# Modulation products in the attention stage: two more weight buffers, loads on GpSimd's queue tied to the present unit, products two half tiles behind

## The chip, the cores and the metric

The kernel runs on one core of a Trainium2 chip. The metric is the device time of one execution in microseconds (us). The core has the engines TensorE (PE in the profile, its weight loads PEld), VectorE (DVE), ScalarE (ACT), GpSimd (POOL) and SyncE (SP, which only issues transfers here). Each takes its instructions in a fixed order, and an instruction whose inputs or whose buffer is not ready holds up all that stand behind it on the same engine.

## The reference, cut to what matters

One layer for 512 latent tokens and 256 context tokens of width 2048, in fp32: a normalisation modulated by the vector `c`, one input projection, four heads of gated linear attention beside a gated convolution, an output projection, and a gated feed-forward network.

```python
mx = jax.nn.silu(c) @ w_mod[i] + b_mod[i]            # 2048 -> 6 x 2048
sh1, sc1, gt1, sh2, sc2, gt2 = split(mx, 6)
hx = modulate(rmsnorm(x, norm1_g), sh1, sc1)
q, k, v, g, lf, lb, cb, cc, cx = split_proj(hx @ w_in)
la_f = log_sigmoid(lf @ w_gate_f + b_gate_f) / 16    # forget gates, la_b alike
o_x = gla_bidir(q, k, v, la_f, la_b, s_f, s_b)       # four heads
mix = concat(o_x * silu(g), cb * conv(cc * cx)) @ w_out
x = x + gt1 * mix
h2 = modulate(rmsnorm(x, norm2_g), sh2, sc2)
x = x + gt2 * swiglu(h2)
```

The change concerns the last four of the six parts of `mx` (gt1, sh2, sc2, gt2: 8192 numbers, each a dot product of 2048 terms) and the forget gates of the latent tokens. The four parts are first needed when the output projection is added to `x`, so their computation is spread over the attention stage.

## The kernel before, in words

Weights come from memory as raw fp32 tiles of 128x1024 (512 KB) in a ring of four `raw` buffers (`load_raw`, line 115, on SP's queue). `load_w` (line 121) splits such a tile in two: ScalarE casts it to `whi` (line 102), VectorE computes the rest `wlo` = raw - whi (line 103). `whi` and `wlo` have three buffers each. TensorE then makes three matmuls for each product (`mm3`, line 92). A projection of 128 columns needs two such tiles; `proj_units` (line 465) calls each a unit, and a unit is 24 matmuls of 128x512.

The attention stage is a sequence of three calls of `weave` (line 528): the context's gates and states (`do_ctx`) beside two projections; the latent gates (`do_gates`, line 549) beside `do_g(0)` and `do_conv(0)`; then each of the four heads (`do_gla`, line 557) beside the projections of later heads and of the convolution. One step of `weave` emits one stage of the attention, one unit, and `mod_some(0.85, 64)`.

`mod_some` (line 367) computes the four parts of `mx` on VectorE. The weights `wm2` are laid out as 64 tiles of 128x2048; a tile comes in two halves of 128x1024, and each half is multiplied by the broadcast `cbc` = silu(c) and summed along its row by one instruction (line 374, `tensor_tensor_reduce`; the profile names it CUSTOM_DVE_ANT_0, and a second short instruction of the same line reads the sum out to `modacc`). The two halves of a tile are loaded and multiplied one directly after the other, in two `raw` buffers of the same ring that the unit weights use, on the same SP queue. Below, "product" means this VectorE instruction of line 374 unless matmuls are named.

Inside a head, TensorE's order is fixed by the program: the score matmuls into `psc` (line 598), VectorE's masked copy of them (line 599, `copy_predicated` into `hbig`), the state updates `pd` (line 618) which reuse a PSUM bank that the masked copy frees, `sn` on VectorE (line 621), `sm` on ScalarE (line 613), and the outputs `po` (line 625). The order of all instructions on each engine is fixed when the program is built; the transfer queues start what stands in them in order.

Scratch for `do_ctx` comes from a pool `hcpool`; it is closed after the context (line 537), and a pool `gp` is opened for gates and heads (line 541). The loop over the heads is at lines 669 to 675, the rest of the modulation at 676 to 679.

Of the kernel before, what the change touches and what calls it, by code (L numbers as in the profile page):

```python
# [7 lines left out]
F32 = mybir.dt.float32  # L8
# [3 lines left out]
ALU = mybir.AluOpType  # L12

P = 128
# [39 lines left out]
def tile_hybrid_block(  # L54
# [14 lines left out]

    es_ep = ExitStack()  # L70
    epool = es_ep.enter_context(tc.tile_pool(name="epool", bufs=1, side="right"))


    def big(dtype=F32):
# [40 lines left out]
    def load_raw(src):  # L115
        n = src.shape[-1]
        r = wpool.tile([P, 1024], F32, tag="raw", name="raw", bufs=4)
        nc.sync.dma_start(r[:, :n], src)
        return r[:, :n]

    def load_w(src, k, eng=None):

        r = load_raw(src)
        n = r.shape[-1]
        hi = wpool.tile([P, 1024], F32R, tag="whi", name="whi", bufs=3)
        lo = wpool.tile([P, 1024], F32R, tag="wlo", name="wlo", bufs=3)
        split(hi[:, :n], lo[:, :n], r, eng)
        return (hi[:, :n].rearrange("p (k n) -> p k n", k=k),
                lo[:, :n].rearrange("p (k n) -> p k n", k=k))
# [34 lines left out]
    gsc2 = cpool.tile([P, KD], F32, name="gsc2")  # L164
    cbc = epool.tile([P, D], F32, name="cbc")
    cstt = epool.tile([P, NBLK, P], F32, name="cstt")
    gatet = epool.tile([33, 2, 512], F32, name="gatet")
    lfT = epool.tile([33, SEQ + CTX], F32, name="lfT")
    maskt = epool.tile([P, 2, SEQ], U8, name="maskt")
    ident, ones, one16 = cidt[:, B_ID, :], cidt[:, B_ONE, :], cstt[:, B_ONE16, :]  # L170
    onecol = cidt[:, B_ONE, 0:1]
# [1 line left out]

    es_hc = ExitStack()
    hcpool = es_hc.enter_context(tc.tile_pool(name="hcpool", bufs=1, side="right"))

    ccolt = hcpool.tile([P, KD, 2], F32, name="ccolt")  # L180
    silsh = hcpool.tile([P, 2, KD, 32], F32, tag="lg", name="silsh")
# [182 lines left out]
    nc.scalar.activation(cbc, cbc, AF.Silu)  # L364
    nmod, owed = [0], [0.0]

    def mod_some(n, last):

        owed[0] += n
        while owed[0] >= 1 and nmod[0] < last:  # L370
            j = nmod[0]
            for hf in range(2):
                w = load_raw(wm2[j][:, hf * 1024 : hf * 1024 + 1024])
                nc.vector.tensor_tensor_reduce(  # L374
                    out=w, in0=w, in1=cbc[:, hf * 1024 : hf * 1024 + 1024], scale=1.0, scalar=0.0,
                    op0=ALU.mult, op1=ALU.add, accum_out=modacc[:, j, hf : hf + 1])
            nmod[0] += 1
            owed[0] -= 1

    MOD_STEP = 0.85  # L380

# [83 lines left out]
    def proj_units(acc, wsrc, x, units=(0, 1), part=ALL):  # L465

        for n, u in enumerate(units):
            w = load_w(wsrc[u], 8)
            for k in range(8):
                mm3(acc[:, part], sl(w, ALL, k), sl(x[8 * u + k], ALL, part), n == 0 and k == 0, n == 1 and k == 7)  # L470
            yield
# [62 lines left out]
            mod_some(MOD_STEP, 64)  # L534

    weave(do_ctx(), (None for g in (do_q(0), do_q(1)) for _ in g))
    es_hc.close()


    es_g = ExitStack()  # L540
    gp = es_g.enter_context(tc.tile_pool(name="gp", bufs=1, side="right"))
    msk = []
    for d in range(2):
        t = hbig()
# [4 lines left out]
    def do_gates():  # L549
        for tt in range(NX):  # L550
            pzs = [bank("pzs") for _ in range(2)]
            for d in range(2):
                mm(pzs[d], tok(lfT, tt), gatet[:, d, :], True, True)
            log_gates(gp, "on", pzs, [las[0][tt], las[1][tt]])
            yield

    def do_gla(h):
# [108 lines left out]
        mix[8 + c] = y  # L666

    weave(do_gates(), (None for g in (do_g(0), do_conv(0)) for _ in g))
    for h in range(HEADS):
        fill = [do_conv(c) for c in (2 * h, 2 * h + 1) if c]  # L670
        if h + 1 < HEADS:
            fill.insert(0, do_g(h + 1))
        if h + 2 < HEADS:
            fill.insert(0, do_q(h + 2))
        weave(do_gla(h), (None for g in fill for _ in g))
    mod_some(64, 64)
    mod_finish(0, 64)
    nc.vector.tensor_scalar(gsc2, modv[:, 32:48], 1.0, None, op0=ALU.add)
    nc.vector.tensor_tensor(gsc2, gsc2, colt[:, C_G2 : C_G2 + KD], op=ALU.mult)
# [570 lines left out]
```

## Time and profile before

| | before |
|---|---|
| median of the 3 runs shown | 2343.65 us (2339.64 to 2347.67) |
| the profiled execution's own time | 2345.66 us |
| its span, first to last instruction | 2343.9 us |
| PE, PEld, DVE, ACT, POOL busy (whole span) | 96%, 76%, 71%, 43%, 6% |
| mean granted TensorE clock | 0.987 |
| first and last product of line 374 | 304.6 and 829.5 us |

How to read it: times in views are microseconds from the span's start. A row of a wait view gives the waiting instruction, the one that released it, the total, the number of times and the longest. In a timeline row, `[3.06 <-DVE hbig L599]` says that the engine stood idle for 3.06 us until VectorE's instruction of line 599 on tile `hbig` ended. PEclk is the share of TensorE's full clock that was granted. A view by windows gives busy time, with the number of instructions in brackets, for each stretch.

### The profile page before, as it was taken

The numbers are of one execution on the slowest core, as the hardware profiler recorded it, in microseconds if no ns is written. First come the engines' busy times: TensorE is split into PE (matmuls) and PEld (weight loads), VectorE is DVE, ScalarE is ACT, GpSimd is POOL, SyncE is SP. The second block draws the span as 40 slices with busy tenths as digits, with TensorE's granted clock in tenths as the row PEclk, the third lists the DMA queues.
The fourth block names the chain that finished last, engine by engine and source line by source line (L and its number), as shares of the span: only waits on it lengthen the run. The fifth ranks groups of instructions, "written<-read, shape, count | busy, mean of one in ns | idle before, by whom it ended". The sixth has DMA issues, their size and how long they took to land.

```text
span 2343.9 us, 27639 instructions
## 1 busy us (share of the span) xinstructions
PE 2253.0 (96%) x10232; PEld 1792.7 (76%) x10232; DVE 1666.7 (71%) x2046; ACT 1010.0 (43%) x1361; POOL 146.1 (6%) x190
## 2 busy tenths in 40 slices
PE   8999999899989999989999999999999999999996
PEld 4765667787867778768888888888888878888875
DVE  3566164655655757779888788878887867787888
ACT  3432155233232334485554555455545544433343
POOL 2433000000000000010000000000000000000001
PEclk9999999999989999999999999999999999999998
DMA  9774365665666654534434643464345585755634
GB/s 323 232 247 135 135 226 169 199 196 191 214 190 192 203 177 163 177 136 135 153 123 147 207 144 123 147 206 144 124 146 207 187 317 177 279 180 197 243 127 143
DMA packets 161619, 431.43 MB, mean 184 GB/s; under 512 B 17867, under 2 KB 38635, under 8 KB 161356
## 3 DMA queue, kind: packets, MB, share of 16 engines
q1 hardware_dynamic: 141612, 380.87, 49.1%
q0 software_dynamic: 8720, 28.58, 3.2%
q10 hardware_dynamic: 11152, 20.21, 2.3%
q8 instruction: 81, 1.33, 0.2%
q14 instruction: 54, 0.44, 0.1%
HBM read 380.82 MB, written 48.78 MB: 183 GB/s over the span
## 4 chain that ended last, share of the span: by engine, by line
PE 51%; DVE 5%; issue 1%; ACT 1%; POOL 0%; DMA 0%; POOLq 0%; SPq 0%; DVEq 0%; ACTq 0%
PE acc L90 50%; DVE wlo L103 2%; PE pt L996 1%; DMA raw<-wd 0%; DVE ch L812 0%; POOL out L1129 0%; DVE y L1108 0%; DVE ch L793 0%; ACT whi L102 0%; ACT h L924 0%; ACT big L909 0%; DVE y L1120 0%; DVE y L1119 0%; DVE u L832 0%; POOL hbig L907 0%
## 5 line engine op out<-in xcount | busy, mean ns | idle before, releaser
L102 ACT CAST whi<-ch 128x1024 fp32r<-128x1024 f32 x350 | 368.8, 1054 | 426.5 <-PE acc L90 362.5
L103 DVE TENSOR_TENSOR wlo<-ch,whi 128x1024 fp32r<-128x1024 f32 x350 | 426.0, 1221 | 135.9 <-ACT whi L102 134.7
L102 ACT CAST whi<-raw 128x1024 fp32r<-128x1024 f32 x252 | 264.2, 1052 | 421.9 <-PE acc L90 221.4
L103 DVE TENSOR_TENSOR wlo<-raw,whi 128x1024 fp32r<-128x1024 f32 x252 | 308.9, 1227 | 187.1 <-ACT whi L102 186.8
L374 DVE CUSTOM_DVE_ANT_0 raw<-raw,cbc 128x1024 f32<-128x1024 f32 x128 | 156.4, 1224 | 193.6 <-DMA raw<-wm 190.8
L90 PE MATMUL acc<-hhl,whi 128*128 128x512 f32 x640 | 200.4, 394 | 0.0
L90 PE MATMUL acc<-hhi,wlo 128*128 128x512 f32 x320 | 135.2, 424 | 16.0 <-DVE wlo L103 15.2
L90 PEld LDWEIGHTS acc<-hhl,whi 128*128 128x128 f32 x640 | 121.3, 190 | 27.7 <-issue 2.5
L90 PE MATMUL acc<-hlo,whi 128*128 128x512 f32 x320 | 127.6, 399 | 0.2 <-DVE hlo L108 0.2
L90 PE MATMUL acc<-whi,a5l 128*128 128x512 f32 x312 | 122.2, 392 | 5.7 <-DVE a5l L103 5.7
L90 PE MATMUL acc<-hhl,wlo 128*128 128x512 f32 x320 | 127.6, 399 | 0.0
L90 PE MATMUL acc<-hhi,whi 128*128 128x512 f32 x320 | 126.7, 396 | 0.0
L90 PE MATMUL acc<-wlo,a0h 128*128 128x512 f32 x312 | 123.3, 395 | 2.1 <-DVE wlo L103 2.1
L90 PE MATMUL acc<-wlo,a6h 128*128 128x512 f32 x312 | 121.6, 390 | 1.4 <-DVE wlo L103 1.4
L90 PE MATMUL acc<-whi,a0h 128*128 128x512 f32 x312 | 122.2, 392 | 0.0
L90 PE MATMUL acc<-whi,a6l 128*128 128x512 f32 x312 | 121.5, 390 | 0.7 <-ACT whi L102 0.4
L90 PE MATMUL acc<-wlo,a5h 128*128 128x512 f32 x312 | 122.0, 391 | 0.0
L90 PE MATMUL acc<-whi,a5h 128*128 128x512 f32 x312 | 121.8, 391 | 0.0
L90 PE MATMUL acc<-whi,a0l 128*128 128x512 f32 x312 | 121.8, 391 | 0.0
L90 PE MATMUL acc<-whi,a6h 128*128 128x512 f32 x312 | 121.4, 389 | 0.0
L90 PE MATMUL acc<-whi,a2l 128*128 128x512 f32 x280 | 108.9, 391 | 4.8 <-ACT whi L102 4.8
L90 PE MATMUL acc<-wlo,a2h 128*128 128x512 f32 x280 | 109.9, 393 | 1.2 <-DVE wlo L103 1.2
(307 smaller groups left out, 4749.5 us busy)
## 6 DMA issues: line engine op xcount, KB each, us to landing
raw<-wm SPq DMA_DIRECT2D x128, 512.0 KB, 4.8
raw<-wu SPq DMA_DIRECT2D x92, 512.0 KB, 4.4
ch<-wu SPq DMA_DIRECT2D x88, 512.0 KB, 3.9
raw<-wc SPq DMA_DIRECT2D x48, 512.0 KB, 3.8
raw<-wd SPq DMA_DIRECT2D x47, 512.0 KB, 6.0
ch<-wd SPq DMA_DIRECT2D x44, 512.0 KB, 5.8
opd<-oh ACTq DMA_DIRECT2D x77, 256.0 KB, 3.1
opd<-ol POOLq DMA_DIRECT2D x77, 256.0 KB, 3.3
```

What stands on the lines that cost most here:

```text
L90: nc.tensor.matmul(o, l, r, start=start, stop=stop, skip_group_check=True)
L102: nc.scalar.copy(hi, src)
L103: (eng or nc.vector).tensor_tensor(lo, src, hi, op=ALU.subtract)
L374: nc.vector.tensor_tensor_reduce(out=w, in0=w, in1=cbc[:, hf * 1024 : hf * 1024 + 1024], scale=1.0, scalar=0.0, op0=ALU.mult, op1=ALU.add, ...
L996: nc.tensor.transpose(pt[:, (2 * i + t) * P : (2 * i + t) * P + P], acts[j][2 * hf + t][:, q * P : q * P + P], ident)
```

## The change

It does five things.

1. `mod_some` now counts halves instead of whole tiles (`owed` grows by 2 x 0.85 = 1.7 a step), and a half may be loaded in one step and multiplied in a later one: loaded halves wait in the list `pend`.
2. From the first head on, `behind` is 2: a half is multiplied only after two later halves have been loaded.
3. From the first head on, loads are issued on GpSimd's queue instead of SP's. Of three halves two go to a new ring `wm` of two 128x1024 buffers in `gp`, one to the `raw` ring.
4. Ahead of each such load GpSimd copies one column of the present unit's `whi` into the buffer (128x1). The load then can't start before ScalarE has cast the present unit's weights and the buffer is free.
5. The latent gates are made in `hcpool`, in the tile that the context's gates used; `gatet` and `lfT` move into `hcpool` as well, which is closed after the gates, and `gp` is opened then.

During the context and the gates `behind` is 0: a half is loaded on SP's queue and multiplied at once, as before, but one half at a time. With 0.85 a step, about 27 halves fall in these 16 steps, and GpSimd issues the remaining 101.

```diff
-    gatet = epool.tile([33, 2, 512], F32, name="gatet")
-    lfT = epool.tile([33, SEQ + CTX], F32, name="lfT")
+    gatet = hcpool.tile([33, 2, 512], F32, name="gatet")
+    lfT = hcpool.tile([33, SEQ + CTX], F32, name="lfT")
...
+    pend, behind, unit = [], [0], []
+
     def mod_some(n, last):
-        owed[0] += n
-        while owed[0] >= 1 and nmod[0] < last:
-            j = nmod[0]
-            for hf in range(2):
-                w = load_raw(wm2[j][:, hf * 1024 : hf * 1024 + 1024])
-                nc.vector.tensor_tensor_reduce(
-                    out=w, in0=w, in1=cbc[:, hf * 1024 : hf * 1024 + 1024], scale=1.0, scalar=0.0,
-                    op0=ALU.mult, op1=ALU.add, accum_out=modacc[:, j, hf : hf + 1])
-            nmod[0] += 1
+        owed[0] += 2 * n
+        while owed[0] >= 1 and (pend or nmod[0] < 2 * last):
             owed[0] -= 1
+            if nmod[0] < 2 * last:
+                j, hf = divmod(nmod[0], 2)
+                src = wm2[j][:, hf * 1024 : hf * 1024 + 1024]
+                if behind[0] and nmod[0] % 3:
+                    w = gp.tile([P, 1024], F32, tag="wm", name="wm", bufs=2)
+                    nc.gpsimd.tensor_copy(w[:, 0:1], unit[0])
+                    nc.gpsimd.dma_start(w, src)
+                elif behind[0]:
+                    w = wpool.tile([P, 1024], F32, tag="raw", name="raw", bufs=4)
+                    nc.gpsimd.tensor_copy(w[:, 0:1], unit[0])
+                    nc.gpsimd.dma_start(w, src)
+                else:
+                    w = load_raw(src)
+                pend.append((j, hf, w))
+                nmod[0] += 1
+                if len(pend) <= behind[0]:
+                    continue
+            j, hf, w = pend.pop(0)
+            nc.vector.tensor_tensor_reduce(
+                out=w, in0=w, in1=cbc[:, hf * 1024 : hf * 1024 + 1024], scale=1.0, scalar=0.0,
+                op0=ALU.mult, op1=ALU.add, accum_out=modacc[:, j, hf : hf + 1])
...
             w = load_w(wsrc[u], 8)
+            unit[:] = [w[0][:, 0, 0:1].bitcast(F32)]
...
-            log_gates(gp, "on", pzs, [las[0][tt], las[1][tt]])
+            log_gates(hcpool, "lg", pzs, [las[0][tt], las[1][tt]])
...
     weave(do_gates(), (None for g in (do_g(0), do_conv(0)) for _ in g))
+    es_hc.close()
+    es_g = ExitStack()
+    gp = es_g.enter_context(tc.tile_pool(name="gp", bufs=1, side="right"))
+    behind[0] = 2
...
-    mod_some(64, 64)
+    mod_some(128, 64)
```

How the instructions stand, at three places. VectorE's order before, in the first head, around the masked copy (line 599); line 374 is the product on a `raw` tile `raw<-raw,cbc` and its read-out `modacc`, line 103 the `wlo` of a unit, line 621 the state update:

```order
L374 ISA raw,modacc<-raw,cbc 128x1024
L374 ISA modacc 128x1
L103 TENSOR_TENSOR wlo<-raw,whi 128x1024
L374 ISA raw,modacc<-raw,cbc 128x1024
L374 ISA modacc 128x1
L374 ISA raw,modacc<-raw,cbc 128x1024
L374 ISA modacc 128x1
L599 COPY_PREDICATED hbig<-maskt,psc 128x512 x2
L621 SCALAR_TENSOR_TENSOR sn<-s_2609,dc,pd 128x256
L601 TENSOR_TENSOR big<-hbig 128x512
L621 SCALAR_TENSOR_TENSOR sn<-s_2609,dc,pd 128x256
```

The same place on VectorE in the changed kernel, where line 395 is the product, line 107 the `wlo`, line 616 the masked copy, line 638 the state update, and `wm` the new ring:

```order
L395 ISA wm,modacc<-wm,cbc 128x1024
L395 ISA modacc 128x1
L107 TENSOR_TENSOR wlo<-raw,whi 128x1024
L395 ISA raw,modacc<-raw,cbc 128x1024
L395 ISA modacc 128x1
L616 COPY_PREDICATED hbig<-maskt,psc 128x512
L107 TENSOR_TENSOR wlo<-raw,whi 128x1024
L616 COPY_PREDICATED hbig<-maskt,psc 128x512
L638 SCALAR_TENSOR_TENSOR sn<-s_2609,dc,pd 128x256
L618 TENSOR_TENSOR big<-hbig 128x512
L638 SCALAR_TENSOR_TENSOR sn<-s_2609,dc,pd 128x256
```

Between the unit's `wlo` and the first masked copy stand two products before and one now, and the next unit's `wlo` has moved in between the two masked copies. The products that stand here now were loaded two halves earlier.

Directly behind the second `sn` of that place, VectorE's order in the changed kernel goes on so (`sn<-sn` is the next step's state update):

```order
L395 ISA wm,modacc<-wm,cbc 128x1024
L395 ISA modacc 128x1
L395 ISA wm,modacc<-wm,cbc 128x1024
L395 ISA modacc 128x1
L395 ISA raw,modacc<-raw,cbc 128x1024
L395 ISA modacc 128x1
L638 SCALAR_TENSOR_TENSOR sn<-sn,dc,pd 128x256 x2
```

Three products now stand between the two steps of the state; before there are a `wlo` and two products between them.

SyncE's queue before, in the first head: the weights of projections (`wq`, `wg`, `wc`) and those of the modulation (`wm`) alternate in the `raw` ring.

```order
L118 DMA raw<-wq 128x1024
L118 DMA raw<-wm 128x1024 x2
L118 DMA raw<-wg 128x1024
L118 DMA raw<-wm 128x1024 x2
L118 DMA raw<-wg 128x1024
```

GpSimd's queue in the changed kernel at its beginning in the heads: `COPY` is the column of the unit's `whi`, `DMA` the load (lines 386 and 387 for the `raw` ring, 382 and 383 for the `wm` ring).

```order
L386 COPY raw<-whi 128x1
L387 DMA raw<-wm 128x1024
L382 COPY wm<-whi 128x1 x2
L383 DMA wm<-wm 128x1024 x2
L386 COPY raw<-whi 128x1
L382 COPY wm<-whi 128x1
L387 DMA raw<-wm 128x1024
L383 DMA wm<-wm 128x1024
L382 COPY wm<-whi 128x1
L383 DMA wm<-wm 128x1024
```

SyncE keeps only the projections' weights in the heads; the modulation's loads stand on GpSimd's queue, where a load can stand behind the column copy of the next one. TensorE's order of instructions is the same in both kernels.

More of the change, by code (lines that the diff above doesn't have):

```diff
@@ L71, in tile_hybrid_block @@
     epool = es_ep.enter_context(tc.tile_pool(name="epool", bufs=1, side="right"))
+    es_hc = ExitStack()
+    hcpool = es_hc.enter_context(tc.tile_pool(name="hcpool", bufs=1, side="right"))
     def big(dtype=F32):
@@ L172, in tile_hybrid_block @@
     selt = smt[:, S_SEL : S_SEL + 2]
-    es_hc = ExitStack()
-    hcpool = es_hc.enter_context(tc.tile_pool(name="hcpool", bufs=1, side="right"))
     ccolt = hcpool.tile([P, KD, 2], F32, name="ccolt")
@@ L536, in tile_hybrid_block @@
     weave(do_ctx(), (None for g in (do_q(0), do_q(1)) for _ in g))
-    es_hc.close()
-    es_g = ExitStack()
-    gp = es_g.enter_context(tc.tile_pool(name="gp", bufs=1, side="right"))
     msk = []
```

## The prediction

> **What bounds the kernel now.** I read the busy times first, then a view by windows of the stage that the change touches, then who waited for whom there, then the two engines' timelines at one gap.
>
> The page's first part, and the windows: the attention stage from the second latent gate to the last head, six stretches inside it, and the rest of the kernel.
>
> ```profile
> PE 2253.0 (96%) x10232; PEld 1792.7 (76%) x10232; DVE 1666.7 (71%) x2046; ACT 1010.0 (43%) x1361; POOL 146.1 (6%) x190
> ...
> core 0: us, PE busy (x) PEld busy (x) DVE busy (x) ACT busy (x) POOL busy (x), PEclk, DMA share, GB/s
> 376.00:832.00 456.00, 420.20 (x1897) 343.83 (x1896) 272.99 (x461) 144.14 (x230) 0.00 (x0) 0.97 0.62 195
> 392.00:400.00 8.00, 6.64 (x22) 5.37 (x23) 3.60 (x4) 2.42 (x4) 0.00 (x0) 0.79 0.64 200
> 452.00:460.00 8.00, 6.24 (x19) 4.54 (x20) 5.66 (x10) 2.90 (x4) 0.00 (x0) 0.79 0.68 201
> 652.00:660.00 8.00, 3.89 (x14) 3.54 (x15) 5.97 (x13) 4.27 (x5) 0.00 (x0) 0.57 0.57 197
> 668.00:680.00 12.00, 9.80 (x30) 7.32 (x31) 7.76 (x14) 3.39 (x6) 0.00 (x0) 0.72 0.50 140
> 780.00:792.00 12.00, 8.13 (x26) 6.12 (x25) 10.21 (x20) 2.56 (x5) 0.00 (x0) 0.72 0.59 191
> 828.00:836.00 8.00, 6.44 (x21) 5.18 (x22) 7.84 (x15) 3.47 (x9) 0.00 (x0) 0.79 0.81 264
> 832.00:2343.00 1511.00, 1470.34 (x6548) 1211.10 (x6546) 1213.93 (x1315) 728.88 (x913) 66.17 (x113) 0.99 0.50 173
> ```
>
> TensorE is the bound, and in this stage it stands idle for 456.00 - 420.20 = 35.8 us. No other engine is full there: VectorE works 273 of 456 us, the transfers 62%, GpSimd does nothing. The six stretches are those where the clock fell: a busy TensorE at 0.79 has lost 0.21 of that time. Busy time times missing clock gives 1.4 + 1.3 + 1.7 + 2.7 + 2.3 + 1.4 = 10.8 us. So the stage holds 35.8 + 10.8 = 46.6 us that better order could return, and no more.
>
> Who waited in that stage, TensorE first, then VectorE, then SyncE's queue; total, times, longest:
>
> ```profile
> PE acc L90 <- DVE wlo L103: 10.9, 9, 2.5
> PE pd L90 <- DVE hbig L599: 10.4, 4, 3.9
> PE po L90 <- ACT sm L613: 5.5, 7, 1.7
> PE psc L90 <- DVE ke L582: 5.2, 1, 5.2
> PE psc L90 <- DVE qe L580: 2.1, 2, 1.4
> PE psc L90 <- ACT a0h L102: 1.7, 1, 1.7
> ...
> DVE raw L374 <- DMA raw<-wm: 172.9, 77, 5.2
> ...
> SPq L118 <- DVE modacc L374: 267.9, 91, 7.0
> SPq L118 <- DVE wlo L103: 71.6, 53, 3.5
> ```
>
> The six rows of TensorE add up to the 35.8 us, and all but 7.2 us of them name VectorE. VectorE in turn stood 172.9 us before products whose weights had not landed, 2.2 us each time. And the loads were late because SyncE's queue waited 267.9 us for a `raw` buffer that an earlier product still held. The circle is closed: a product frees a buffer, only then its successor is loaded, and VectorE has already arrived at the successor.
>
> One place shows what this does to TensorE: VectorE, then TensorE, in the first head.
>
> ```profile
> 444.62 1.22 DVE L103 TENSOR_TENSOR wlo<-raw,whi 128x1024 fp32r<-128x1024 f32 x1
> 450.19 1.23 DVE L374 CUSTOM_DVE_ANT_0 raw<-raw,cbc 128x1024 f32<-128x1024 f32 x1 [4.35 <-DMA raw<-wm]
> 452.61 1.33 DVE L599 COPY_PREDICATED hbig<-maskt,psc 128x512 f32<-128x512 uint8 x2
> ...
> 449.03 0.39 PE L90 MATMUL acc<-hlo,whi 128*128 128x512 f32 x1
> 449.26 0.39 PE L90 MATMUL acc<-hhi,whi 128*128 128x512 f32 x1
> 453.38 1.13 PE L90 MATMUL pd<-vx,kk 128*128 128x256 f32 x4 [3.06 <-DVE hbig L599]
> 457.33 0.63 PE L90 MATMUL acc<-hlo,whi 128*128 128x512 f32 x1
> ```
>
> The score matmuls were long done when the masked copy began at 452.61. It stood behind a product that waited 4.35 us for its weights, and TensorE stood 3.06 us for the copy. After the gap a matmul takes 0.63 us; ahead of it they take 0.39 us and start 0.23 us apart.
>
> **The change part by part.** *Products two halves behind, more buffers.* Work is the same: 128 products of 1.22 us, and as many bytes. What changes is how long before its use a half is loaded. These are the other gaps of TensorE on which the sum rests, and three waits of VectorE just ahead of them:
>
> ```profile
> 393.36 0.69 PE L90 MATMUL acc<-hhi,wlo 128*128 128x512 f32 x1 [2.46 <-DVE wlo L103]
> 409.28 1.23 DVE L374 CUSTOM_DVE_ANT_0 raw<-raw,cbc 128x1024 f32<-128x1024 f32 x1 [3.96 <-DMA raw<-wm]
> 413.25 0.50 PE L90 MATMUL acc<-hhi,wlo 128*128 128x512 f32 x1 [1.68 <-DVE wlo L103]
> 650.22 1.22 DVE L374 CUSTOM_DVE_ANT_0 raw<-raw,cbc 128x1024 f32<-128x1024 f32 x1 [2.78 <-DMA raw<-wm]
> 743.20 0.50 PE L90 MATMUL acc<-hhi,wlo 128*128 128x512 f32 x1 [2.07 <-DVE wlo L103]
> 827.13 1.23 DVE L374 CUSTOM_DVE_ANT_0 raw<-raw,cbc 128x1024 f32<-128x1024 f32 x1 [2.31 <-DMA raw<-wm]
> 829.56 0.50 PE L90 MATMUL acc<-hhi,wlo 128*128 128x512 f32 x1 [2.26 <-DVE wlo L103]
> ...
> L374 DVE CUSTOM_DVE_ANT_0 raw<-raw,cbc 128x1024 f32<-128x1024 f32 x108 | 132.2, 1224 | 173.8 <-DMA raw<-wm 172.9 <-DVE modacc L374 0.4
> L103 DVE TENSOR_TENSOR wlo<-raw,whi 128x1024 fp32r<-128x1024 f32 x64 | 78.0, 1219 | 5.4 <-ACT whi L102 5.4
> ```
>
> 64 units in 456 us make 7.1 us a unit; with 1.7 halves a step, two halves are 8.4 us. A load lands 4.8 us after its issue (below). So a half that is issued when the present unit has been cast has about 8.4 us until VectorE wants it, and some 2 us are left after copy, issue and landing. Row by row of the 35.8 us, what I expect to stay:
>
> - `hbig`, 10.4 us: the wait of 4.35 us ahead of the masked copy is longer than the gap of 3.06 us behind it, so without it the copy is done in time. The next unit's `wlo` now stands between the two copies (1.2 us); that fits into the 5.5 us of matmuls (24 at 0.23 us apart) that TensorE has in between. 0.9 us stays.
> - `wlo`, 10.9 us: the gap at 393 lies in the gates, where halves are still loaded and multiplied at once, and stays with 2.4 us. The gaps at 413 and 829 stand behind waits of 3.96 and 2.31 us for weights and go. That at 743 I take to go with them. 1.0 us stays of these 8.4.
> - `ke`, 5.2 us: 2.78 of it is the wait at 650, and one product less may stand there. 1.5 us stays.
> - `qe` and `a0h`, 3.8 us: nothing in the change shortens these chains. All stays.
> - `sm`, 5.5 us: the chain `pd`, `sn`, `sm`, `po` has its own length; what products put between stays partly. I keep half, 2.7 us.
>
> That leaves 0.9 + 2.4 + 1.0 + 1.5 + 3.8 + 2.7 = 12.3 us, and 23.5 go. As no gap but that at 393 then reaches the 2.26 us after which the clock fell (it did not after 2.07), 1.4 us of clock loss stay, and 0.8 for one new gap; 8.6 go.
>
> *Loads on GpSimd, tied to the unit.* The nearest rows, from the page's sixth part and from the tile view of the stores that GpSimd already issues in the feed-forward stage:
>
> ```profile
> raw<-wm SPq DMA_DIRECT2D x128, 512.0 KB, 4.8
> ...
> opd<-oh ACTq DMA_DIRECT2D x77, 256.0 KB, 3.1
> opd<-ol POOLq DMA_DIRECT2D x77, 256.0 KB, 3.3
> ...
> L1010 POOL DMA_DIRECT2D opd<-ol x77: 539/539/556, 1136.2 to 1949.2; - x77
> ```
>
> An issue takes GpSimd 0.54 us and a store lands 0.2 us later than one from ScalarE's queue. 101 loads make 55 us on an engine that is empty there, so their own time costs nothing. No row shows a load of 512 KB from this queue, nor a 128x1 copy; I take 4.8 + 0.2 us for the one. The copy's cost is between nothing, under idle time, and the 1.2 us of the longest VectorE instruction that it could stand beside; I take 0.3. Two things wait on this queue: a load behind the column copy of the next half, and that copy behind the product that frees its buffer. Then a half is issued only when the product two before it is done, and 8.4 us shrink by VectorE's unevenness. At the place with three products in a row the third may be late, with `sn` behind it. I charge 1.5 us in all, between 0 and 6 (one late half of 1.5 us a head).
>
> SyncE's queue loses the 101 loads, so the projections' weights no longer stand behind them; of 2.7 buffers a step in the `raw` ring 1.6 remain. Rows show no cost of that while `whi` is cast ahead: no gain is counted.
>
> *Gates in the first pool.* The same instructions in another tile; the pool that the heads use opens later, while the gates' last reader is several units back. I cost it at nothing; without that cover it would be one wait at the first head, of about the 2.46 us seen at 393.
>
> *Sum.* 23.5 + 8.6 - 1.5 = 30.6 us. On the profiled execution's own 2345.66 us (its span of 2343.9 and 1.8 around it) that gives 2315.1; that execution is 2.0 us above the median of the runs shown, so on the median's scale 2343.65 - 30.6 = 2313.
>
> The Trainium skill (page "TensorE: Matmul & The Clock Gate", section "Part 1: The HAM clock gate") has the clock fall only after an idle window of about 3.4 us. By it only the gaps of 5.2 and 3.9 us would have cost clock, 1.7 + 2.3 = 4.0 us instead of 10.8, and the sum would be near 25 us, 2318 us. The trace shows the clock at 0.79 after gaps of 2.46 and 2.26 us too, so the sum keeps 10.8.
>
> **The rivals.** *Loads still late.* A load now waits for the unit's cast, for a buffer and for the queue ahead of it, so VectorE could go on waiting for half of its 172.9 us. TensorE would keep about half of its 46.6 us: 2343.65 - 23 = 2320. For it speaks the thin 2 us; against it, that two halves of lead exceed the longest wait seen, 5.2 us, by far. Chance 0.15.
>
> *GpSimd and VectorE in each other's way.* If each column copy and each issue waited for a VectorE instruction of 1.2 us, a load would come 2.4 us later, the 2 us would be gone, and products would wait about 1.2 us each, 101 x 1.2 = 121 us instead of 172.9: a third less, and a third of 30.6 us, so 2333. VectorE is busy 60% of the stage. Against it: the 77 issues took 539 to 556 ns while VectorE was busy 1213.93 of 1511 us. Chance 0.06. The Trainium skill ("SBUF — State Buffer", section "SBUF: two separate sides") states such a lock: a VectorE instruction with two SBUF inputs, which products and `wlo` are, shuts out a GpSimd instruction that reads SBUF for its whole length, and the reverse. No row here shows it yet.
>
> *Nothing is gained.* The gaps go over to the chains `qe`, `sm` and ScalarE's casts, which were late together with VectorE, and TensorE waits as long under other names: 2343 give or take 6. Against it: the waits for weights stand directly ahead of the gaps. Chance 0.05.
>
> *Slower: the projections' weights come late.* A third of the halves, 34, still sit in the `raw` ring, now from the column copy until two halves later. The `raw` ring turns round in order, so the unit load that gets such a buffer waits for that product. `whi` has three buffers, so a unit may be cast up to two units, 14.2 us, early; if a product is over that late, TensorE stands. If each of the 34 cost 1.5 us, it would be 51 us against 30.6: 2364. Against it: the hold is some 12 us, and three more buffers remain. Chance 0.06.
>
> **How the numbers follow.** The forecast has the remaining 0.68: 2313. Its best case is that only the gap at 393 stays, 46.6 - 3.8 = 42.8 us, 2301; with 2 us for the spread of runs, the low end is 2299. The high end takes in the two cases of smaller gain, 2333. Left out are the last two, 0.11, and the forecast's tails. A measurement of this kernel can tell about 0.3%, 7 us, from no change. Faster: 0.68 + 0.15 + 0.06 less 0.02 for tails, 0.87. Same 0.06, slower 0.07.
>
> **What would show it.** In the profile after: VectorE's wait for `wm` weights in the heads falls from 172.9 to under 40 us; the rows `pd` on `hbig` and `acc` on `wlo` fall to some 5 us together; the clock stays at full outside the gates; attention ends about 30 us earlier, and the rest keeps its 1511 us. It is wrong if the waits for weights on VectorE stay above 90 us, if ScalarE's casts wait for the projections' loads, or if GpSimd's queue shows long copies.

## The result and the profile after

The changed kernel takes 2310.91 us (median of 4 runs, 2308.36 to 2315.25), the kernel before on the same chip 2345.66 us (2339.64 to 2349.25): 0.9853 of it, with a 95% interval of 0.9837 to 0.9869. The forecast was 2313 us.

| | before | changed |
|---|---|---|
| median of the runs, us | 2345.66 | 2310.91 |
| span of the profiled execution, us | 2343.9 | 2309.4 |
| granted clock over the span | 0.987 | 0.991 |
| from the gates' last `pzs` to `ptr`, us | 468.6 | 432.7 |

The page's first part, in the changed kernel:

```profile
PE 2237.2 (97%) x10232; PEld 1785.9 (77%) x10232; DVE 1665.1 (72%) x2046; ACT 1011.0 (44%) x1361; POOL 250.8 (11%) x392
```

TensorE does the same 10232 matmuls in 15.8 us less busy time (2253.0 before). To place the gain I cut both traces at the same two instructions: the gates' last `pzs` matmul, and `ptr`, which turns the finished modulation into rows. The windows view of before, between these two and from there to the end (span, then busy time and count of TensorE, its weight loads, VectorE, ScalarE, GpSimd, then granted clock, share of the transfers, GB/s):

```profile
373.60:842.20 468.60, 432.80 (x1947) 353.50 (x1946) 283.76 (x480) 153.12 (x249) 0.00 (x0) 0.97 0.61 194
842.20:2343.90 1501.70, 1460.14 (x6507) 1202.84 (x6505) 1203.73 (x1296) 722.28 (x897) 66.17 (x113) 0.99 0.51 174
```

The same two stretches in the changed kernel:

```profile
372.20:804.90 432.70, 415.94 (x1947) 345.64 (x1946) 277.34 (x468) 152.06 (x242) 104.57 (x202) 0.99 0.61 209
804.90:2309.40 1504.50, 1462.51 (x6506) 1203.96 (x6506) 1208.86 (x1308) 722.99 (x901) 66.29 (x113) 0.99 0.51 173
```

The stretch starts 1.4 us earlier, is 35.9 us shorter, and the rest is 2.8 us longer: 1.4 + 35.9 - 2.8 = 34.5 us, the difference of the spans. Of the 35.9 us, 19.0 are idle time of TensorE (468.60 - 432.80 = 35.8 before, 16.8 after), and 16.9 are busy time: the same 1947 matmuls take 415.94 instead of 432.80 us.

Who kept TensorE waiting from the last gate on (total, times, longest), in the changed kernel:

```profile
PE ptr L888 <- DVE modv L403: 8.2, 1, 8.2
PE acc L94 <- DVE wlo L107: 6.7, 4, 2.1
PE po L94 <- ACT sm L630: 1.8, 3, 1.2
```

The rows of `hbig`, `ke`, `qe` and `a0h` are gone altogether. Half of what is left is one new gap. VectorE's own waits in the same stretch (372.2 to 804.9 us) did not go the same way:

```profile
DVE wm L395 <- DMA wm<-wm: 93.8, 30, 8.6
DVE raw L395 <- DMA raw<-wm: 49.0, 19, 5.6
```

That is 142.8 us, where before had 172.9. VectorE still waits for weights; inside the heads TensorE hardly feels it. The timeline of the changed kernel's first head, at the place that the prediction quotes, shows how (VectorE's rows, then one of TensorE):

```profile
431.83 1.23 DVE L107 TENSOR_TENSOR wlo<-raw,whi 128x1024 fp32r<-128x1024 f32 x1 [1.02 <-ACT whi L106]
438.65 1.23 DVE L395 CUSTOM_DVE_ANT_0 raw<-raw,cbc 128x1024 f32<-128x1024 f32 x1 [5.59 <-DMA raw<-wm]
439.80 0.73 DVE L616 COPY_PREDICATED hbig<-maskt,psc 128x512 f32<-128x512 uint8 x1
440.42 1.21 DVE L107 TENSOR_TENSOR wlo<-raw,whi 128x1024 fp32r<-128x1024 f32 x1
441.55 0.73 DVE L616 COPY_PREDICATED hbig<-maskt,psc 128x512 f32<-128x512 uint8 x1
...
444.47 1.02 PE L94 MATMUL pd<-vx,kk 128*128 128x256 f32 x4
```

A product still waits 5.59 us for its weights directly ahead of the masked copy, longer than the 4.35 us of before. But only one product stands there now, and it ends at 439.80; the copies are done at 442.3, and `pd` starts at 444.47 without a wait. Before, two products stood between the `wlo` and the copy, and `pd` waited 3.06 us.

The new gap lies at the end of the stretch (timeline of the changed kernel, VectorE, then TensorE):

```profile
788.35 1.23 DVE L395 CUSTOM_DVE_ANT_0 wm<-wm,cbc 128x1024 f32<-128x1024 f32 x1 [6.00 <-DMA wm<-wm]
799.04 1.23 DVE L395 CUSTOM_DVE_ANT_0 wm<-wm,cbc 128x1024 f32<-128x1024 f32 x1 [3.72 <-DMA wm<-wm]
804.60 0.22 DVE L403 TENSOR_TENSOR modv<-modv,colt 128x64 f32<-128x64 f32 x1
...
804.88 0.59 PE L888 MATMUL ptr<-cidt,modv 128*16 128x128 f32 x2 [8.19 <-DVE modv L403]
807.03 0.63 PE L94 MATMUL acc<-whi,a0l 128*128 128x512 f32 x1
```

The last products are late, `modv` with them, and TensorE stands 8.19 us for it; afterwards a matmul takes 0.63 us for a while.

GpSimd in the changed kernel, first the tile view of the new ring (shortest, median, longest ns):

```profile
L382 POOL COPY wm<-whi x67: 180/501/1242, 411.0 to 793.1; 128x1 f32<-128x1 f32 x67
```

Two of the copies in its timeline:

```profile
431.86 1.24 POOL L386 COPY raw<-whi 128x1 f32<-128x1 f32 x1 [6.23 <-ACT whi L106]
433.04 0.18 POOL L382 COPY wm<-whi 128x1 f32<-128x1 f32 x1
```

And the list of transfers (KB each, us from issue to landing):

```profile
wm<-wm POOLq DMA_DIRECT2D x67, 512.0 KB, 5.7
```

A copy of 128x1 takes 0.18 us alone and 1.24 us when it starts with VectorE's `wlo` of 431.83. A load lands 5.7 us after its issue (median), 0.9 us later than from SyncE's queue before.

### The profile page after: what moved, and what is told of

Read it like the earlier page. It is cut to its first block, busy times and chain, and to the rows that moved or that the text cites. A ratio compares the mean times of both kernels' runs of the same rounds, so it can differ in the third digit from the quotient of the medians.

```text
span 2309.4 us, 27908 instructions
## 1 busy us (share of the span) xinstructions
PE 2237.2 (97%) x10232; PEld 1785.9 (77%) x10232; DVE 1665.1 (72%) x2046; ACT 1011.0 (44%) x1361; POOL 250.8 (11%) x392
## 4 chain that ended last, share of the span: by engine, by line
issue 56%; POOL 2%; PE 1%; DVE 1%; POOLq 0%; ACT 0%; DVEq 0%; ACTq 0%
POOL opd L1031 2%; PE acc L94 1%; POOL out L1150 0%; DVE wlo L107 0%; POOL hbig L928 0%; DVE ch L833 0%; DVE u L985 0%; POOL xnd L988 0%; ACT whi L106 0%; DVE hbig L986 0%; DVE u L853 0%; POOLq L1031 0%; POOLq L1267 0%; POOLq L1150 0%; DVE rs_t L151 0%
## 5 line engine op out<-in xcount | busy, mean ns | idle before, releaser
L395 DVE CUSTOM_DVE_ANT_0 wm<-wm,cbc 128x1024 f32<-128x1024 f32 x67 | 81.4, 1224 | 94.4 <-DMA wm<-wm 93.8
L1031 POOL DMA_DIRECT2D opd<-ol x77 | 41.8, 543 | 889.3 <-DVE ol L107 889.2
L395 DVE CUSTOM_DVE_ANT_0 raw<-raw,cbc 128x1024 f32<-128x1024 f32 x61 | 74.4, 1223 | 65.7 <-DMA raw<-wm 65.3
```

Of the source, the lines that this page charges most:

```text
L395: nc.vector.tensor_tensor_reduce(out=w, in0=w, in1=cbc[:, hf * 1024 : hf * 1024 + 1024], scale=1.0, scalar=0.0, op0=ALU.mult, op1=ALU.add, ...
L1031: nc.gpsimd.dma_start(opd[j][i, 1].rearrange("p k t -> p (k t)"), lo.bitcast(F32))
```

## The experiments

Theory: the gain comes from the lead that the lag of two halves and the extra buffers give a load. Rival: it comes from the pace and place of the products on VectorE, which the tie to the unit sets when the program is ordered, and the lag has no part in it. TensorE's order of instructions is the same in all versions but the last, which moves `ptr`. All ratios are against the kernel before on the same chip. The table puts the twelve versions together; its stretch is the one cut above, from the last `pzs` to `ptr`, with TensorE's idle time in it from the windows view, and the last column counts, from VectorE's order, the products between a `wlo` and the masked copy that follows it, for the first of the two masked copies in each of the four heads. Waits are those in each version's own stretch.

| version | us | ratio (95%) | stretch, us | idle, us | products |
|---|---|---|---|---|---|
| before | 2342 to 2346 | 1 | 468.6 | 35.8 | 7 |
| the change | 2310.91 | 0.9853 (0.9837 to 0.9869) | 432.7 | 16.8 | 3 |
| halves and gates only | 2336.53 | 0.9957 (0.9942 to 0.9972) | 456.1 | 31.0 | 7 |
| change without lag | 2310.64 | 0.9849 (0.9820 to 0.9878) | 432.3 | 14.5 | 3 |
| change without the `wm` ring | 2353.40 | 1.0029 (1.0015 to 1.0044) | 468.1 | 37.3 | 3 |
| change without tie | 2347.22 | 1.0011 (0.9999 to 1.0022) | 469.0 | 37.5 | 7 |
| SyncE, no tie, no lag | 2329.69 | 0.9942 (0.9926 to 0.9959) | 451.8 | 25.3 | 6 |
| SyncE, tie, no `wm` ring, no lag | 2321.16 | 0.9907 (0.9887 to 0.9927) | 440.4 | 18.4 | 3 |
| SyncE, tie, `wm` ring, lag | 2295.42 | 0.9792 (0.9778 to 0.9807) | 415.4 | 1.9 | 1 |
| SyncE, tie, `wm` ring, no lag | 2294.72 | 0.9797 (0.9780 to 0.9813) | 418.2 | 4.4 | 1 |
| `wm` on SyncE, `raw` on GpSimd | 2319.17 | 0.9900 (0.9881 to 0.9918) | 434.2 | 16.0 | 3 |
| `raw` on SyncE, `wm` on GpSimd | 2315.32 | 0.9894 (0.9859 to 0.9928) | - | - | 3 |
| modulation a little faster | 2315.91 | 0.9869 (0.9841 to 0.9898) | 434.3 | 13.2 | 3 |
| `ptr` two units later | 2316.70 | 0.9885 (0.9871 to 0.9900) | - | - | 3 |

Two stretches are left out: one profiled execution (2328.65 us) was the longest of its four, 13 us over their median, and in the other version `ptr` stands elsewhere. With the second copies counted too, the last column has 4 for the change, 6 without the lag, and 1 and 3 for the two versions that show 1.

### Halves and gates only

Lag, rings, tie and GpSimd's queue are out; a half is loaded on SyncE's queue and multiplied at once, through the heads too.

```diff
-    behind[0] = 2
```

> Parts 1 and 5 alone: modulation halves one at a time, gates in the first pool; all loads on SyncE's queue in the raw ring, each product directly after its load. If the gain comes from earlier loads on another queue (lead theory), this is within 8 us of the kernel before (ratio 0.997 to 1.003), TensorE idle in the stage stays near 35 us. If spreading the products one by one is what keeps VectorE from arriving late at the masked copies, it already gains 10 us or more (ratio below 0.996).

Measured: 2336.53 us, 0.9957, just under the 0.996 named for the pace of the products. TensorE's waits in this version:

```profile
PE pd L94 <- DVE hbig L616: 13.7, 4, 5.3
```

The row of `hbig` is no smaller than before (13.7 us beside 10.4), so the two small parts do not help it. They give 0.43% of the change's 1.47%.

### The lag away

```diff
-                if len(pend) <= behind[0]:
+                if len(pend) <= 0:
```

> The changed kernel with products directly behind their load in the program (no lag of two); the new ring, GpSimd's queue and the column copies stay. Lag theory: VectorE then stands about 5 us before every product, over 300 us in the stage, TensorE waits as before or more: ratio 0.995 to 1.02. Weight-lead theory (what counts is that the projections' weights no longer stand behind modulation loads, so that casts and wlo run ahead): most of the gain stays, ratio below 0.990.

Measured: 2310.64 us, 0.9849 (0.9820 to 0.9878), beside the change's 0.9853. TensorE's and VectorE's waits:

```profile
PE ptr L888 <- DVE modv L403: 6.5, 1, 6.5
...
DVE wm L395 <- DMA wm<-wm: 94.2, 28, 8.5
DVE raw L395 <- DMA raw<-wm: 48.8, 21, 5.5
```

VectorE waits 143.0 us without the lag and 142.8 with it. The lag of the program is worth nothing that these runs can tell; the theory of the lead falls as far as it rests on the lag. VectorE's order hardly differs: ahead of the 40th, 50th and 60th `wlo` of the kernel stand 28, 45 and 62 products with the lag and without it. The ordering puts the products late by itself.

### The `wm` ring away

Tie, lag and GpSimd's queue stay; all halves go through the `raw` ring.

```diff
-                if behind[0] and nmod[0] % 3:
+                if False:
```

> The changed kernel without the two new buffers: all halves of the heads in the raw ring, lag of two, GpSimd's queue and column copies kept. Lag theory: the lag stays, so the gain stays, ratio 0.985 to 0.989. Weight-lead theory: three held halves leave one raw buffer for the projections' weights, casts wait for their loads, and the gain is lost or turned: ratio above 0.997, ScalarE's waits for projection loads above 100 us in the stage.

Measured: 2353.40 us, 1.0029. What ScalarE's casts waited for, in this version:

```profile
ACT whi L106 <- DMA raw<-wc: 125.0, 26, 11.3
ACT whi L106 <- DMA raw<-wg: 50.7, 9, 9.2
ACT whi L106 <- DMA raw<-wq: 21.4, 3, 10.7
```

The projections' weights come late, 197.1 us of waits for them (52.7 before, 42.2 in the change), and ScalarE, then VectorE's `wlo`, then TensorE are late behind them. The places of the products are those of the change, 3 in the table. So the extra buffers are needed, and what they do is to keep the modulation's halves out of the way of the projections' weights.

### The tie away

The column copies are out, at both places; rings, lag and GpSimd's queue stay.

```diff
-                    nc.gpsimd.tensor_copy(w[:, 0:1], unit[0])
```

> The changed kernel without the column copies: a load on GpSimd's queue starts as soon as its buffer is free. If the tie to the present unit is what keeps loads out of each other's way, the projections' loads land later and ScalarE's casts lag: ratio 0.988 to 0.995. If the tie is idle (buffers alone pace the loads, copies up to 1.2 us long are only cost), ratio 0.982 to 0.987, VectorE's waits for modulation weights fall from 156 to under 100 us.

Measured: 2347.22 us, 1.0011 (0.9999 to 1.0022): the whole gain is gone, more than either expectation allowed. Late weights, which the first one named, do not show: ScalarE's casts wait 6.6 us for the projections' loads, and 42.2 in the change. VectorE waits less for weights than in any version above, and TensorE waits more; their waits:

```profile
PE acc L94 <- DVE wlo L107: 17.5, 10, 6.1
PE pd L94 <- DVE hbig L614: 6.0, 2, 3.9
...
DVE wm L393 <- DMA wm<-wm: 72.1, 37, 4.9
DVE raw L393 <- DMA raw<-wm: 66.7, 28, 4.5
```

The groups of products from 376 to 650 us (busy, mean ns, idle before), without the tie:

```profile
L393 DVE CUSTOM_DVE_ANT_0 wm<-wm,cbc 128x1024 f32<-128x1024 f32 x67 | 81.5, 1224 | 72.2 <-DMA wm<-wm 72.1
L393 DVE CUSTOM_DVE_ANT_0 raw<-raw,cbc 128x1024 f32<-128x1024 f32 x24 | 29.4, 1224 | 16.9 <-DMA raw<-wm 16.7
```

and in the change:

```profile
L395 DVE CUSTOM_DVE_ANT_0 wm<-wm,cbc 128x1024 f32<-128x1024 f32 x40 | 48.6, 1224 | 53.8 <-DMA wm<-wm 53.4
L395 DVE CUSTOM_DVE_ANT_0 raw<-raw,cbc 128x1024 f32<-128x1024 f32 x27 | 33.0, 1224 | 39.7 <-DMA raw<-wm 39.5 <-POOL raw L386 0.2
```

Without the tie 91 products fall into this time, with it 67. It is the same by place in VectorE's order: ahead of the 60th `wlo` of the kernel stand 94 products without the tie, 62 with it and 66 before. Loads that depend on nothing but a free buffer pull the products forward, three between two `wlo` and three ahead of a masked copy (7 in the table, as before). The tie paces them. That the crowding is what costs the gain is read from TensorE's waits for `wlo` and `hbig`; no run changes VectorE's order alone.

### The extra buffers alone, on SyncE's queue

No tie, no lag.

```diff
-                    nc.gpsimd.tensor_copy(w[:, 0:1], unit[0])
-                    nc.gpsimd.dma_start(w, src)
+                    nc.sync.dma_start(w, src)
...
-                if len(pend) <= behind[0]:
+                if len(pend) <= 0:
```

> Only the two more buffers are left of the change in the heads (beside halves and gates): two of three halves in the new ring, loads on SyncE's queue without copies, products directly after their load. Buffer theory (the projections' weights are cast ahead because the raw ring is no longer filled by modulation halves): most of the gain, ratio 0.984 to 0.990, casts that wait for TensorE 70 us or more in the stage. Queue theory (projections' loads must not stand behind modulation loads in one queue): ratio 0.993 to 1.000, casts waiting for TensorE under 55 us.

Measured: 2329.69 us, 0.9942, which the intervals do not separate from halves and gates alone (0.9957). Buffers without the tie are worth little.

### The tie alone, on SyncE's queue

No `wm` ring, no lag.

```diff
-                if behind[0] and nmod[0] % 3:
+                if False:
...
-                    nc.gpsimd.dma_start(w, src)
+                    nc.sync.dma_start(w, src)
...
-                if len(pend) <= behind[0]:
+                if len(pend) <= 0:
```

> The kernel before with halves, gates in the first pool and the column copy as the only other change: raw ring of four alone, loads on SyncE's queue, no lag. Tie theory (pacing products by the unit is the whole effect): ratio below 0.987. Buffers and tie both needed: above 0.993, ScalarE's casts waiting over 100 us for projection loads.

Measured: 2321.16 us, 0.9907, between the two ranges expected: 0.5% under halves and gates alone, with intervals apart. ScalarE still waits 95.1 us for `wc` and 29.9 for `wg` here. Tie and buffers together, on the same queue (below), reach 0.9797. So each gives little without the other, 0.5% and 0.15%, and both give 1.6%: the tie puts the products in place, the buffers keep the projections' weights on time. This version and the one without the `wm` ring (2353.40) differ in queue and lag; which of the two makes the 1.2% between them was not tried.

### Everything but GpSimd's queue

GpSimd still copies the column; the load is issued by SyncE.

```diff
-                    nc.gpsimd.dma_start(w, src)
+                    nc.sync.dma_start(w, src)
```

> The changed kernel with column copies, ring and lag as they are, but the loads issued on SyncE's queue. Each then holds up the projections' loads behind it until the present unit is cast. Queue theory: ratio above 0.995. Buffer theory: a small loss, 0.986 to 0.991.

Measured: 2295.42 us, 0.9792 (0.9778 to 0.9807), the best of all versions, 0.6% under the change; both theories had expected a loss. Its windows row:

```profile
371.20:786.60 415.40, 413.47 (x1946) 346.25 (x1944) 280.62 (x471) 151.16 (x241) 55.21 (x101) 1.00 0.65 218
```

TensorE's and VectorE's waits:

```profile
PE acc L94 <- DVE wlo L107: 1.5, 1, 1.5
PE ptr L888 <- DVE modv L403: 0.5, 1, 0.5
DVE wm L395 <- DMA wm<-wm: 68.0, 35, 4.5
DVE raw L395 <- DMA raw<-wm: 23.3, 17, 2.8
```

One row of its transfers:

```profile
wm<-wm SPq DMA_DIRECT2D x67, 512.0 KB, 4.7
```

TensorE stands still for 2 us in the whole stretch, at a clock of 1.00, and VectorE still waits 91.3 us for weights: its idle time costs nothing when what TensorE needs next stands ahead of it. The ordering put only one product between a `wlo` and a head's first masked copy here; in the first head the one that stands there in the change has moved behind the state update. The loads land 1.0 us sooner. GpSimd's copies take as long as in the change (55.21 us of GpSimd for 101 copies; in the change 40.0 and 13.1 us for the two rings), so it is not their length that costs the change its 0.6%. What their place costs is another matter. GpSimd takes its instructions in order, so a load whose own column is copied stands behind the copy for a later half, and that copy waits for a product. GpSimd's timeline of the changed kernel, near the end of the heads:

```profile
784.06 0.19 POOL L386 COPY raw<-whi 128x1 f32<-128x1 f32 x1
...
789.64 1.12 POOL L382 COPY wm<-whi 128x1 f32<-128x1 f32 x1 [4.57 <-DVE modacc L395]
790.70 0.53 POOL L387 DMA_DIRECT2D raw<-wm  x1
```

The load of 790.70 belongs to the column copied at 784.06: it is issued 6.45 us after that copy ends. Over the 101 halves of the change this delay adds up to 117.7 us, 1.2 us each and 7.26 us at the longest; with all loads on SyncE's queue it adds up to 11.5 us.

The same without the lag:

```diff
-                    nc.gpsimd.dma_start(w, src)
+                    nc.sync.dma_start(w, src)
...
-                if len(pend) <= behind[0]:
+                if len(pend) <= 0:
```

> Tied loads on SyncE's queue, two more buffers, but products directly behind their load in the program. If the lag does nothing (the builder puts products where loads are estimated to have landed, with or without it): within 0.002 of the kernel with lag, 0.977 to 0.982. If the lag matters once the queue is quick: 0.983 or more.

Measured: 2294.72 us, 0.9797. Again the lag does nothing.

### The queues mixed

First the `wm` ring on SyncE and the `raw` third on GpSimd (line 383), then the reverse (line 387), each with this edit at its line:

```diff
-                    nc.gpsimd.dma_start(w, src)
+                    nc.sync.dma_start(w, src)
```

> The changed kernel with only the loads of the new ring (two of three) issued on SyncE's queue; the third, into the raw ring, stays on GpSimd's. VectorE's order at build is almost that of the changed kernel, so this isolates the queue at run time. If the 0.6% by which all tied loads on SyncE beat the changed kernel come from the queue of the many loads: ratio 0.979 to 0.982. If they come from how long the raw ring is held by halves that GpSimd loads late: ratio stays near 0.985.

> The reverse: only the loads into the raw ring (one of three) on SyncE's queue, the new ring's on GpSimd's. If the time that halves hold the raw ring is what costs: ratio 0.979 to 0.982, SyncE waits less than 236 us for products. If the queue of the many loads is what costs: near 0.985.

Measured: 2319.17 us (0.9900) and 2315.32 us (0.9894); neither is better than the change, and the first lies outside both ranges expected, though in it two thirds of the loads are on the faster queue. The transfers of the first:

```profile
wm<-wm SPq DMA_DIRECT2D x67, 512.0 KB, 4.4
raw<-wm POOLq DMA_DIRECT2D x34, 512.0 KB, 6.6
```

The 67 loads that land in 4.4 us gain nothing here. But products are taken in a fixed order, the other third lands in 6.6 us, and VectorE waits 99.6 us for it instead of 49.0, so these versions do not rule out landing time. Nor do they separate out the delay behind column copies, which is 30.4 us in the first and 67.2 in the second. In both, the table counts 3 products, as in the change, and the versions with 1 are those at 0.979; that suggests that VectorE's order has a part in it. Without any column copy GpSimd's queue is slower too (1.0011 without the tie beside 0.9942 on SyncE, in another order of VectorE). No run holds the order fixed while the queue changes with all the loads, so what makes the 0.6% stays open.

### The gap at the end

The modulation a little faster in the heads, so that it ends ahead of the attention:

```diff
+    MOD_STEP = 0.95
```

> The changed kernel with 0.95 instead of 0.85 tiles a step in the heads, so that the modulation ends about seven steps before the last head does. If the new gap of 8.2 us at the end (TensorE's transposes of the gates wait for the modulation's last products) is a true cost, it goes and with it some 2 us of low clock: 8 to 11 us less than the changed kernel, ratio about 0.981 to the kernel before. If the gap only hides another wait, or more products a step crowd VectorE in the heads, the ratio stays at 0.984 to 0.988.

Measured: 2315.91 us, 0.9869. The gap at `ptr` is gone, and others come back; TensorE's waits:

```profile
PE acc L94 <- DVE wlo L107: 5.2, 5, 1.5
PE pd L94 <- DVE hbig L616: 3.7, 2, 2.5
```

The stretch from the last `pzs` to `ptr` is 434.3 us, 1.6 more than in the change: what the end wins, the heads lose. Its ordering differs ahead of that stretch too, whose start is 4.5 us later (the last `pzs` at 376.7 instead of 372.2), and most of the difference of the spans lies there. The intervals of the two ratios overlap, so this version is not shown to be slower than the change.

Then TensorE's `ptr` itself, moved behind two more units of the projection that follows:

```diff
-    gt1d, gt2d = cols_to_row(0, "gt1"), cols_to_row(48, "gt2")
+    gts = {}
+
+    def rows_out():
+        gts[0], gts[48] = cols_to_row(0, "gt1"), cols_to_row(48, "gt2")
...
+            third = before[0, 0, 2]
+            before[0, 0, 2] = lambda: (third(), rows_out())
```

> The changed kernel with TensorE's two transposes of the gates (which waited 8.2 us for the modulation's last products) placed behind the third weight tile of the output projection instead of ahead of the first, some 11 us later in TensorE's order. If that gap is a true cost: 8.2 us and about 2 us of low clock less, ratio about 0.981. If something else waits there for the same products (operands, gate rows for the residual), the gap moves and the ratio stays near 0.985.

Measured: 2316.70 us, 0.9885. TensorE's timeline at that place:

```profile
800.61 0.79 PE L94 MATMUL acc<-wlo,a0h 128*128 128x512 f32 x1 [7.54 <-DVE wlo L107]
813.69 0.38 PE L888 MATMUL ptr<-cidt,modv 128*16 128x128 f32 x2
830.21 1.22 PE L94 MATMUL acc<-whi,a5l 128*128 128x512 f32 x2 [5.24 <-ACT whi L106]
```

This is no faster than the change either: 0.9885 beside 0.9853. `ptr` waits for nothing, and the gap stands in front of the first `wlo` of the next projection instead, with a second one of 5.24 us behind it, which waits for a cast of ScalarE. What is late first at the end of the heads is VectorE, whichever instruction of TensorE asks first. Of the tied versions with the `wm` ring, the gap went without others in its place only where all loads are on SyncE's queue (0.5 us with the lag, 1.1 without).

## Why the prediction was right in size, and where it was wrong

**The total** of 30.6 us stands against 34.5 measured on the spans. It was right by a sum whose terms were not: 23.5 us of idle time forecast and 19.0 measured, 8.6 us of clock forecast and 16.9 us of busy time measured. That these errors have opposite signs is luck.

**The step that failed** is the lead: that a half issued two halves ahead "has about 8.4 us until VectorE wants it", so that VectorE's waits fall from 172.9 to under 40 us. They are 142.8 us, beyond the 90 that I had named as the mark of being wrong, and the run without the lag has 143.0 us and the same time. In its place the runs show two things that hold only together. The tie keeps the ordering from crowding products in front of what TensorE waits for (without it 1.0011). The extra buffers keep the modulation's halves from holding up the projections' weights (without them 1.0029). I saw both parts in the diff and took the tie for a condition on loads alone, which at best costs nothing.

**Row by row.** `hbig` to 0.9 us: it is 0, but not for the reason given, since the product ahead of the copy waits longer than before (5.59 against 4.35 us); one product less stands there, as the order showed. `ke` 1.5, `qe` and `a0h` 3.8: all 0. `sm` 2.7: 1.8. `wlo` 3.4: 6.7, of which the gap in the gates is 1.93 us where 2.4 were forecast. Without the new gap 8.5 us of idle time would be left, not the 12.3 forecast. That `qe` and `a0h` went too was not in any of my reasons: I had taken them for chains of their own.

**The new gap**, 8.2 us at `ptr`, was in no term and no rival. The modulation's end now falls behind the attention's: the last `modv` comes at 804.60, when TensorE has been waiting for 8 us. I asked what was late next inside the heads and not at their end.

**The clock** was mis-sized: 8.6 us forecast, 16.9 us of busy time measured for the same matmuls. The bound of 46.6 us "and no more" took the missing clock on the busy time of six stretches, 10.8 us. The version with 1.9 us of idle time does the same work (1946 of the 1947 records) in 413.47 us of busy time instead of 432.80, so before holds 19.3 us there, and idle and busy time together 35.8 + 19.3 = 55.1 us. The granted clock of 0.97 over 468.6 us accounts for some 14 us of the 19.3 (an estimate, 0.03 x 468.6); what makes the rest was not measured apart.

**GpSimd** at 1.5 us, between 0 and 6: with the loads on SyncE's queue the kernel is some 15 us faster (2295.42 against 2310.91), so the queue's whole price was outside my bounds, even if part of it is the order that comes with it. The landing grew by 0.9 us, not 0.2; the median copy of the `wm` ring takes 0.5 us, not 0.3. The prediction named the wait of a load behind the next half's column copy and priced it with the rest at 1.5 us; the delay adds up to 117.7 us over 101 loads, though no run shows how much of it TensorE pays.

**The rivals.** *Loads still late*: VectorE waited on, more than the rival said, but in the rows of which the rival speaks TensorE kept 8.5 of its 35.8 us, not half. The link between the two engines' waits, on which that rival and the forecast both rested, does not hold for the sum of them. *GpSimd and VectorE in each other's way*: the copies stretch to 1.24 us, the issues keep a median of 530 ns (at most 544 on the `wm` ring, 708 on the `raw` ring), and VectorE's `wlo` beside a copy takes 1.23 us, as ever. The Trainium skill ("SBUF — State Buffer", section "SBUF: two separate sides") states a lock between a VectorE instruction with two SBUF inputs and a GpSimd instruction that reads SBUF; the 0.18 and 1.24 us of the copy agree with it, in the one direction that the rows show. *Slower by late projection weights*: this mechanism is real, and the extra buffers are what holds it off; without them it makes 2353.40 us.

**The clock's rule.** I had read a threshold out of the gaps of before: the clock fell after 2.26 us and not after 2.07. The changed kernel does not contradict it, with 1.93 us in the gates and 2.12 us in the heads at full clock and 8.19 us at a lowered one. The other runs do. With `raw` on SyncE the clock fell behind a gap of 1.91 us (at 732.75), and with halves and gates only it stayed at full behind one of 2.62 us (at 441.29). The two places in windows of 3.41 us, first the former, then the latter:

```profile
729.94:733.35 3.41, 1.50 (x12) 1.22 (x11) 3.41 (x5) 1.35 (x2) 1.08 (x3) 1.00 0.77 256
733.35:736.76 3.41, 3.41 (x10) 2.63 (x9) 3.37 (x6) 3.04 (x5) 1.16 (x2) 0.50 0.46 145
...
437.10:440.51 3.41, 1.57 (x11) 1.26 (x10) 3.41 (x9) 1.36 (x3) 0.00 (x0) 1.00 0.74 193
440.51:443.92 3.41, 2.63 (x17) 2.49 (x17) 1.24 (x3) 1.51 (x2) 0.00 (x0) 1.00 0.72 257
```

In the traces here, between 300 and 860 us, the low clock comes in pieces of 3.41 us that start on a fixed grid of 3.41 us. Every piece of that grid at full clock in which TensorE was idle for 1.94 us or more is followed by one at 0.50, and none with less than 1.64 us is; in between it went both ways. The gap of 1.91 us lies in one piece, that of 2.62 us across two. So the step from a gap's length to the clock failed, and where a gap falls on the grid counts as well. The Trainium skill ("TensorE: Matmul & The Clock Gate", section "Part 1: The HAM clock gate") gives an idle window of about 3.4 us; in these traces some 1.9 us of such a window was enough. The measurement decides, and the sum that followed the page, 25 us, is further from the 34.5 than the one that followed the trace.

## What to carry to other kernels

A wait on an engine that is not the bound is worth what stands behind it: count the instructions between it and what the bound engine needs next, and compare orders, before taking the wait itself for the price. A data dependence on a load (here a column of the present unit) paces everything that follows from it when a program is ordered, and buffers without such a pace can cost all that they bring. When work is spread over a stage, look where its last piece falls.

## What the hardware showed unexpectedly

A GpSimd copy of 128x1, which takes 0.18 us alone, takes up to 1.24 us beside a VectorE instruction of 1.23 us with two inputs, and the VectorE instruction is not longer for it. A load of 512 KB on GpSimd's queue landed 5.7 us after its issue, and the same loads on SyncE's queue 4.7 us (medians), beside the same other loads. The clock that TensorE is granted goes by pieces of 3.41 us on a fixed grid: 1.91 us of idle time inside one piece lowered it, 2.62 us across two did not.
